# Gate and up projections of a decoder block: two sums of weight blocks come out of accumulating DMAs, and one attention step holds back its weight splits

## The chip, the core and the metric

The kernel runs on one core of one Trainium2 chip. It computes one whole decoder block in float32. The metric is the device time of one execution in microseconds (us), and the number that counts is the median of several runs. Before the change it is 1122.65 us, from three runs between 1121.96 and 1122.95 us.

The engines are named as in the profile: PE is TensorE, with PEld for its weight loads, DVE is VectorE, ACT is ScalarE, POOL is GpSimd and SP is SyncE. SP and ACT issue ordinary DMAs. POOL issues those that add to their destination.

## The reference, cut to what matters

```python
h = _rmsnorm(x, g_mix_pre)                        # x: 1024 tokens of 1024 features
u_pool, q, k, v, gates = split(h @ w_in + b_in)   # 512, 512, 128, 128, 2048 features
y_pool = multiscale_pool(u_pool)                  # windows 2, 4, 8, 16, then w_pool
y_attn = sliding_window_sink_attention(rotary(q), rotary(k), v)   # window 128, 8 heads of 64
g = sigmoid(gates)
merged = g[:, :1024] * (y_pool @ w_branch_pool) + g[:, 1024:] * (y_attn @ w_branch_attn)
x = x + _rmsnorm(merged @ w_out, g_mix_post)
h2 = _rmsnorm(x, g_mlp_pre)
ff = square(relu(h2 @ w_up)) @ w_down             # 4096 features between
out = x + _rmsnorm(ff, g_mlp_post)
```

## The kernel before, in words

**Products.** Each float32 operand is split into a high part (a cast, on ACT, L101) and a low part (source minus high part, on DVE, L104). A product of two such operands is three matmuls, high by high, high by low and low by high (`PASSES`). The helper `split` (L99) records every such pair of instructions under L101 and L104, so the tiles tell them apart.

**Seven products for eight.** The gate projection (2048 features), the up projection (4096) and the down projection multiply 2 by 2 blocks with seven block products in Winograd's form. For gates and up this is the class `Pairs` (L444). A pair p holds two neighbouring tiles of 128 output features. Its weights are four blocks: A11 and A12 (first tile, first and second half of the 1024 input features) and A21 and A22 (second tile). Each block is 128 by 4 by 128. The activations are four blocks B11 to B22 (input half by token half), and T1 to T4 are sums and differences of them. The seven products are numbered as in `OPERAND` (L442): 1 is A11 by B11, 2 is A12 by B21, 4 is A22 by T4, 5 is S1 by T1, 6 is S2 by T2, 7 is S3 by T3, and 3 is S4 by B22, where before the change S1 = A21 + A22, S2 = S1 - A11, S3 = A11 - A21 and S4 = A12 - S2. One product is 4 blocks of 128 by 3 passes, or 12 matmuls of 128 by 512.

**Where the sums are made.** `load` (L453) fetches one feature tile, 512 KB, on the SP queue, into a staging buffer (`st`, 3 buffers) or a `g` buffer. `operand` (L458) makes one weight operand. For products 5, 6, 7 and 3 it first adds or subtracts weight blocks on DVE: S1 at L464, S2 at L467, S4 at L471 and S3 at L474. These are four 128 by 512 operations for each pair, and there are 8 pairs of gates and 16 of up. S1 and S2 are held in a tile `ws` of the buffer group `ga` (6 buffers), which also holds gate operands (`ar`), raw activations (`xr`) and, in the up stage, operands of B22. `rest` (L505) runs products 6, 7, 5, 4 and 3 and puts the results together on DVE (L512, L519, L523, L526, L532).

**The stages.** (1) Queries, keys and values of the first tokens. (2) Attention, eight steps of 128 queries, while PE is also fed with other matmuls: `fill` (L651) takes them from the generator `others` (L613), which holds the remaining queries, keys and values and the pooling input projection (`u_half`, L571) with small products of branch weights (`wb_half`, L593). (3) Gates: products 1 and 2 of all eight pairs, then the five others pair by pair. (4) Branches, merge and `w_out`. (5) Up, pair by pair. (6) Down. (7) Output.

**What sets the order.** Stages 2 and the first part of 3 stand in `manual_schedule`: PE, DVE and ACT execute exactly in the order written there, and in the first part of the gates SP does so too. Elsewhere, and for POOL everywhere, the framework orders the instructions of each engine itself before the run, by program order and its own estimate of when operands and buffers are ready. In every case an engine's queue is in order: an instruction that waits holds up those behind it.

**The attention step.** In step n (L763 on) the program transposes and splits the probabilities (`attend_t`), starts the scores of step n + 2, makes the masked copy (`attend_own`, L387), scales step n + 1 (`softmax_scale`, L367), runs `fill(3.6)`, finishes the scores and the maximum of step n + 2 (L344, L351), transposes queries and keys of step n + 3 (`post_qkv`, L287: casts on ACT, low parts `qt` and `klo` on DVE), runs `fill(4.2)` and multiplies with the values (`attend_v`, L390, matmuls L399). `post_qkv`, `attend_t` and `attend_v` draw from three PSUM banks tagged `at`. A `u_half` normally splits the next weights at its eighth matmul (`flush(between[th])`, L586). While `held[0]` is true it only notes that this is due (L584). Before the change that holds during `fill(4.2)` and `attend_v` alone, and what is due is made right after `attend_v` (L793). In step 4 the `fill(3.6)` contains such a split: the weights of the next `u_half` (L556).

**Signs.** `build_gate` (L708) and `build_second` (L1049) make T1 to T4 on DVE. `gfin_b` (L1139), a broadcast of the last gain, is loaded at the start of the up stage. It takes one of the two buffers `bc`, and is first read after the third product of the down stage (L1306).

Of the kernel before, what the change touches and what calls it, by code (L numbers as in the profile page):

```python
# [8 lines left out]
F32 = mybir.dt.float32  # L9
# [5 lines left out]
P = 128  # L15
# [35 lines left out]
def block_kernel(ctx: ExitStack, tc, xt, x, consts, vecs, sinks, b_qkv, g_post, g_mlp_post,  # L51
# [100 lines left out]
    cp.tile([P, 40], F32, name="room")  # L152
# [291 lines left out]
    class Pairs:  # L444
# [12 lines left out]

        def operand(self, p, i):  # L458

            r0, r1_ = self.raw[2 * p], self.raw.get(2 * p + 1)  # L460
            if i in (5, 6, 3):
                if p not in self.sums:
                    self.sums[p] = ga_.tile([P, 2, 4, P], F32, tag="ga", name=nm("ws"))
                    dve.tensor_tensor(self.sums[p][:, 0], r1_[:, :4], r1_[:, 4:], ALU.add)  # L464
                src, s2 = self.sums[p][:, 0], self.sums[p][:, 1]
                if i == 6:
                    dve.tensor_tensor(s2, src, r0[:, :4], ALU.subtract)  # L467
                    src = s2
                elif i == 3:
                    src = r0[:, 4:]  # L470
                    dve.tensor_tensor(src, src, s2, ALU.subtract)  # L471
            elif i == 7:
                src = r0[:, :4]
                dve.tensor_tensor(src, r0[:, :4], r1_[:, :4], ALU.subtract)  # L474
            else:
                src = r0[:, :4] if i == 1 else r0[:, 4:] if i == 2 else r1_[:, 4:]
# [28 lines left out]
        def rest(self, p, f1, b6, b7, b5, done=(), then=None, b4=None):  # L505
# [6 lines left out]
            dve.tensor_tensor(u2, u2, b6, ALU.add)  # L512
# [10 lines left out]
            dve.tensor_tensor(f1[:, 512:], v7, b5, ALU.add)  # L523
# [8 lines left out]
            dve.tensor_tensor(u2, u2, b5, ALU.add)  # L532
# [114 lines left out]

    stream = others()
# [59 lines left out]
    def build_gate(kt, place):  # L708
# [21 lines left out]
    with tc.manual_schedule(engines={mybir.EngineType.PE, mybir.EngineType.DVE, mybir.EngineType.Activation}):  # L730
        rsqrt(r1, ssq, NT)
        act.activation(warm, r1[:, :1], AF.Exp)
# [30 lines left out]
        for n in range(NT):  # L763
# [12 lines left out]
            flush(late)  # L776
            fill(3.6)
# [15 lines left out]
            held[0] = False  # L793
            while len(held) > 1:
                flush(between[held.pop()])
# [39 lines left out]
    with tc.manual_schedule(engines={mybir.EngineType.PE, mybir.EngineType.DVE, mybir.EngineType.Activation,  # L835
# [7 lines left out]
        for p in range(NG0):  # L843
# [34 lines left out]
    for p in range(8):  # L878
# [3 lines left out]
        if p > 1:  # L882
            gt.load(2 * p)
            gt.load(2 * p + 1, g32([NK, P]) if p > 2 else None)
# [164 lines left out]
    def build_second(kt):  # L1049
# [8 lines left out]
        dve.scalar_tensor_tensor(r11, b12, gain(kt), r11, ALU.mult, ALU.subtract)  # L1058
        dve.scalar_tensor_tensor(t2, b22, gain(4 + kt), r11, ALU.mult, ALU.subtract)
        dve.scalar_tensor_tensor(t3, b22, gain(4 + kt), t3, ALU.mult, ALU.subtract)  # L1060
# [78 lines left out]
    gfin_b = bcast(g_mlp_post, D)  # L1139
# [20 lines left out]
    up.load(0)  # L1160
    up.load(1)
# [28 lines left out]
    def load_pair(p):  # L1190
        up.load(2 * p)
        up.load(2 * p + 1, g32([NK, P]))

    load_pair(1)
    up.rest(0, ga_.tile([P, S], F32, tag="ga", name="f1_first"), b6, b7, bank("at"), done=(6, 7),
            b4=bank("mm"))
    for p in range(1, NP):
# [16 lines left out]
        if p < NP - 1:  # L1214
            load_pair(p + 1)
# [8 lines left out]
    flush()  # L1224
    fpool.__exit__(None, None, None)
# [233 lines left out]
```

## Time and profile before

| | us |
|---|---|
| median of three runs | 1122.65 (1121.96 to 1122.95) |
| the profiled execution: its own time | 1122.0 |
| its span, first to last instruction | 1120.2 |
| PE busy | 1109.4, 99% of the span |
| PEld, DVE, ACT, POOL busy | 918.0, 791.5, 536.4, 62.3 |
| bytes moved by DMA | 197.41 MB, mean 176 GB/s |

The profile is one execution. Its own time is 1.8 us longer than the span, and 0.65 us below the median. The granted TensorE clock was 0.999. A row of a timeline reads: start in us, duration in us, engine, line, operation, output <- inputs, shapes, count, and in brackets the idle time of the engine just before and what ended it. A row of groups reads: line, engine, operation, tiles, shapes, count, then busy us, mean ns of one, and idle us before. A row of windows reads: the stretch, its length, busy us (and instructions) of PE, PEld, DVE, ACT and POOL, then the granted clock, the busy share of the DMA engines and GB/s. A row of DMA queues gives packets, MB, and the time of the packets as a share of 16 engines' span.

### The profile page before, as it was taken

How to read it: one execution, taken by the hardware profiler on the slowest of the kernel's cores; microseconds unless marked ns; L12 is line 12 of the kernel's file. 1: busy time of each engine (PE TensorE's matmuls, PEld its weight loads, DVE VectorE, ACT ScalarE, POOL GpSimd, SP SyncE). 2: the span in 40 equal slices, each digit the busy share in tenths (PEclk: the TensorE clock that was granted, in tenths of full speed). 3: DMA queues.
4: the chain of work that ended last, by engine and by line, in shares of the span. 5: the costliest groups of instructions: out<-in, count | busy, mean ns of one | idle time of the engine just before them, and what ended most of it. 6: DMA issues, size and time to landing. Idle time of an engine off the chain costs nothing.

```text
span 1120.2 us, 13921 instructions
## 1 busy us (share of the span) xinstructions
PE 1109.4 (99%) x5167; PEld 918.0 (82%) x5167; DVE 791.5 (71%) x1158; ACT 536.4 (48%) x904; POOL 62.3 (6%) x105
## 2 busy tenths in 40 slices
PE   9999999999999999999999999999999999999997
PEld 7888788888888888888888888888888888888885
DVE  5578767899768874448978767666547945447787
ACT  7466656445432333547545646354434445344342
POOL 0333210000000410000000000000000000000000
PEclk9999999999999999999999999999999999999999
DMA  9305669355772543323466554535597766332653
GB/s 349 136 11 137 151 145 311 131 188 207 244 252 69 189 147 127 131 100 115 159 215 252 198 209 157 188 122 182 204 365 249 248 199 188 97 99 71 208 189 109
DMA packets 82483, 197.41 MB, mean 176 GB/s; under 512 B 7152, under 2 KB 19568, under 8 KB 82416
## 3 DMA queue, kind: packets, MB, share of 16 engines
q1 hardware_dynamic: 72448, 174.78, 46.3%
q10 hardware_dynamic: 5616, 19.66, 4.6%
q0 software_dynamic: 4352, 2.10, 1.8%
q8 instruction: 40, 0.66, 0.2%
q14 instruction: 27, 0.22, 0.1%
HBM read 140.94 MB, written 55.57 MB: 175 GB/s over the span
## 4 chain that ended last, share of the span: by engine, by line
PE 92%; DVE 5%; ACT 2%; DMA 1%; issue 1%; DVEq 0%
PE mm L491 24%; PE at L491 16%; PE at L1297 15%; PE mm L1297 12%; PE mm L991 7%; PE mm L428 5%; PE mm L187 3%; PE mm L430 3%; PE mm L581 2%; PE at L196 1%; PE sc L187 1%; PE at L399 1%; PE sc L335 1%; PE mm L196 1%; PE at L1036 1%
## 5 line engine op out<-in xcount | busy, mean ns | idle before, releaser
L1297 PE MATMUL at<-ar,wh 128*128 128x512 f32 x744 | 169.6, 389 | 0.0
L1297 PEld LDWEIGHTS at<-ar,wh 128*128 128x128 f32 x744 | 139.6, 188 | 29.3 <-DVE ar L104 0.4
L1297 PE MATMUL mm<-ar,wh 128*128 128x512 f32 x576 | 131.0, 389 | 0.0
L1297 PEld LDWEIGHTS mm<-ar,wh 128*128 128x128 f32 x576 | 108.1, 188 | 22.4
L104 DVE TENSOR_TENSOR wh<-raw,wh 128x1024 fp32r<-128x1024 f32 x53 | 64.8, 1223 | 80.4 <-ACT wh L101 80.4
L101 ACT CAST wh<-raw 128x1024 fp32r<-128x1024 f32 x53 | 55.8, 1053 | 130.9 <-PE at L1297 58.6
L101 ACT CAST wh<-st 128x512 fp32r<-128x512 f32 (+1 forms) x105 | 66.4, 642 | 79.7 <-PE at L491 21.2
L104 DVE TENSOR_TENSOR wh<-st,wh 128x512 fp32r<-128x512 f32 (+1 forms) x105 | 78.2, 754 | 28.8 <-ACT wh L101 26.5
L491 PE MATMUL mm<-gr,wh 128*128 128x512 f32 x309 | 74.0, 390 | 0.0
L491 PEld LDWEIGHTS mm<-gr,wh 128*128 128x128 f32 x309 | 57.7, 188 | 11.8
L491 PE MATMUL mm<-T,wx 128*128 128x512 f32 x288 | 67.4, 389 | 0.0
L491 PEld LDWEIGHTS mm<-T,wx 128*128 128x128 f32 x288 | 54.1, 188 | 11.2
L491 PE MATMUL at<-T,wx 128*128 128x512 f32 x252 | 59.4, 389 | 0.0
L491 PEld LDWEIGHTS at<-T,wx 128*128 128x128 f32 x252 | 47.3, 188 | 9.8
L491 PE MATMUL mm<-x,wh 128*128 128x512 f32 x240 | 55.2, 389 | 0.0
L491 PEld LDWEIGHTS mm<-x,wh 128*128 128x128 f32 x240 | 45.1, 188 | 9.3
L104 DVE TENSOR_TENSOR ar<-B,ar 128x1024 fp32r<-128x1024 f32 x37 | 45.1, 1219 | 7.0 <-ACT ar L101 6.8
L581 PE MATMUL mm<-x,wh 128*128 128x512 f32 x192 | 47.8, 396 | 0.0
L101 ACT CAST ar<-B 128x1024 fp32r<-128x1024 f32 x37 | 38.9, 1050 | 9.2 <-DMA B<-in_w_dn_dram 6.3
L491 PE MATMUL at<-gr,wh 128*128 128x512 f32 x174 | 42.5, 390 | 0.0
L581 PEld LDWEIGHTS mm<-x,wh 128*128 128x128 f32 x192 | 35.2, 188 | 7.7
L491 PEld LDWEIGHTS at<-gr,wh 128*128 128x128 f32 x174 | 32.6, 188 | 7.3 <-DVE gr L104 0.5
(363 smaller groups left out, 2145.1 us busy)
## 6 DMA issues: line engine op xcount, KB each, us to landing
raw<-f_dram SPq DMA_DIRECT2D x53, 512.0 KB, 3.8
f_dram<-g SPq DMA_DIRECT2D x30, 512.0 KB, 3.3
B<-in_w_dn_dram SPq DMA_DIRECT2D x24, 512.0 KB, 5.8
st<-in_w_up_dram SPq DMA_DIRECT2D x23, 512.0 KB, 3.6
st<-in_w_g_dram SPq DMA_DIRECT2D x18, 512.0 KB, 4.2
f_dram<-g ACTq DMA_DIRECT2D x17, 512.0 KB, 2.6
g<-spill_dram SPq DMA_DIRECT2D x16, 512.0 KB, 4.6
raw<-in_w_dn_dram SPq DMA_DIRECT2D x16, 512.0 KB, 4.7
```

What stands on the lines that cost most here:

```text
L101: act.copy(hi, src)
L104: eng.tensor_tensor(lo, src, f32(hi), ALU.subtract)
L187: pe.matmul(bq, xs_[k][n // 4][:, xh, n % 4 * P:(n % 4 + 1) * P], wq[k][:, h, :], start=k == 0 and j == 0, stop=k == NK - 1 and j == 2)
L196: pe.matmul(bkv_of(n), xs_[k][n // 4][:, xh, n % 4 * P:(n % 4 + 1) * P], wkv[k // 2][:, h, k % 2, :], start=k == 0 and j == 0 and not (joi ...
L335: pe.matmul(sb[:, kv, i, :nk], qt[r, qx, m * P:(m + 1) * P], kx[r, k0:k0 + nk], start=j == 0, stop=j == 2)
L399: pe.matmul(flat(yb), v[:, kv, :], flat(p[:, 4 * kv:4 * kv + 4]), start=j == 0, stop=j == len(mms) - 1)
L428: pe.matmul(bs[th], whi[:, k, :], rhs(k, hl, th), start=k == 0 and hl == 0, stop=False)
L430: pe.matmul(bs[th], wlo[:, k, :], rhs(k, 0, th), start=False, stop=k == nk - 1)
L491: pe.matmul(b, w[:, wh, kt, :], xo[kt][:, xh, :], start=not after and kt == 0 and j == 0, stop=kt == 3 and j == 2, skip_group_check=after)
L581: pe.matmul(b, (whi, wlo)[h][:, k, :], xr(k, xh, th), start=j == 0, stop=j == len(mms) - 1)
L991: pe.matmul(obs[n][dj], l, wos[k][whl][:, dj * 512:(dj + 1) * 512], start=k == 0 and hl == 0 and whl == 0, stop=k == NK - 1 and hl == 1)
L1297: pe.matmul(bs[t], fo[fh][:, k2, t * P:(t + 1) * P], wo_[wh][:, k2, :], start=not after and s2 == 0 and k2 == 0 and j == 0, stop=s2 == NS ...
```

## The change

Three things are changed.

The weight loads: `load_sums(p)` lets POOL issue three DMAs. The first writes A21 twice into both halves of a `ws` tile (512 KB written), the second adds A22 to one half (256 KB) and the third adds A11 to the other (256 KB). This gives S1 = A21 + A22 and S3 = A11 + A21 without DVE. `load_pair` loads A11 and A12 as before, but of the second feature tile only A22. S2 = S1 + A11 and S4 = A12 + S2 stay on DVE. `load_sums` is called two pairs ahead. The signs that come out otherwise go into T1 to T4, with a column of negated gains (`ngain`, two 128 by 8 operations at the start of attention), and into the subtractions in `rest`.

The buffers: a `ws` tile now lives from `load_sums` until its last reader. The first result of up moves from `ga` to `bc`, and `gfin_b` is loaded after the last pair of up.

The attention step: in step 4 `held[0]` is also true during `fill(3.6)` and until after `post_qkv(7)`.

```diff
+    ngain = cp.tile([P, 16], F32, name="ngain")
         def load_sums(self, p):
+            if 2 * p + 1 >= self.src.shape[0]:
+                return
+            q = self.sums[p] = ga_.tile([P, 2, 4, P], F32, tag="ga", name=nm("ws"))
+            a21 = self.src[2 * p + 1][:, :4]
+            pool.dma_start(q, a21.unsqueeze(1).broadcast_to([P, 2, 4, P]))
+            pool.dma_start(q[:, 1], self.src[2 * p + 1][:, 4:], accum_op=ALU.add)
+            pool.dma_start(q[:, 0], self.src[2 * p][:, :4], accum_op=ALU.add)
+        def load_pair(self, p, t=None):
+            self.load(2 * p)
+            t = stage([NK, P]) if t is None else t
+            nc.sync.dma_start(t[:, :4], self.src[2 * p + 1][:, 4:])
+            self.raw[2 * p + 1] = t
         def operand(self, p, i):
-            r0, r1_ = self.raw[2 * p], self.raw.get(2 * p + 1)
-            if i in (5, 6, 3):
-                if p not in self.sums:
-                    self.sums[p] = ga_.tile([P, 2, 4, P], F32, tag="ga", name=nm("ws"))
-                    dve.tensor_tensor(self.sums[p][:, 0], r1_[:, :4], r1_[:, 4:], ALU.add)
-                src, s2 = self.sums[p][:, 0], self.sums[p][:, 1]
-                if i == 6:
-                    dve.tensor_tensor(s2, src, r0[:, :4], ALU.subtract)
-                    src = s2
-                elif i == 3:
-                    src = r0[:, 4:]
-                    dve.tensor_tensor(src, src, s2, ALU.subtract)
-            elif i == 7:
-                src = r0[:, :4]
-                dve.tensor_tensor(src, r0[:, :4], r1_[:, :4], ALU.subtract)
+            r0, r1_, q = self.raw[2 * p], self.raw.get(2 * p + 1), self.sums.get(p)
+            if i == 6:
+                src = r1_[:, 4:]
+                dve.tensor_tensor(src, q[:, 1], r0[:, :4], ALU.add)
+            elif i == 3:
+                src = r0[:, 4:]
+                dve.tensor_tensor(src, src, r1_[:, 4:], ALU.add)
...
 -            dve.tensor_tensor(u2, u2, b6, ALU.add)
+            dve.tensor_tensor(u2, b6, u2, ALU.subtract)
...
-            dve.tensor_tensor(f1[:, 512:], v7, b5, ALU.add)
+            dve.tensor_tensor(f1[:, 512:], v7, b5, ALU.subtract)
...
-            dve.tensor_tensor(u2, u2, b5, ALU.add)
+            dve.tensor_tensor(u2, b5, u2, ALU.subtract)
...
+    def release():
+        held[0] = False
+        while len(held) > 1:
+            flush(between[held.pop()])
...
-        dve.tensor_tensor(a0, a1, a0, ALU.subtract)
-        dve.scalar_tensor_tensor(a1, b1, gb, a1, ALU.mult, ALU.subtract)
-        dve.scalar_tensor_tensor(b1, b1, gb, a0, ALU.mult, ALU.subtract)
+        dve.tensor_tensor(a0, a0, a1, ALU.subtract)
+        dve.scalar_tensor_tensor(a1, b1, ngain[:, 4 + kt:5 + kt], a1, ALU.mult, ALU.add)
+        dve.scalar_tensor_tensor(b1, b1, gb, a0, ALU.mult, ALU.add)
...
         rsqrt(r1, ssq, NT)
+        for i, col in enumerate((V_G, V_GM)):
+            dve.tensor_scalar(ngain[:, 8 * i:8 * i + 8], vec[:, col:col + 8], -1.0, None, ALU.mult)
...
             flush(late)
+            held[0] = n == 4
             fill(3.6)
...
             if n + 3 < NT:
                 post_qkv(n + 3)
+            release()
...
             held[0] = True
             fill(3.0 if n == NT - 1 else 4.2)
             attend_v(n)
-            held[0] = False
-            while len(held) > 1:
-                flush(between[held.pop()])
+            release()
...
             if p + 5 < NG0:
                 gt.load(2 * p + 10)
-            elif p < 5:
-                gt.load(p - 3)
+            elif p == 3:
+                gt.load_sums(0)
+            elif p == 4:
+                gt.load_pair(0)
             elif p == 6:
-                gt.load(2)
-                gt.load(3, g32([NK, P]))
+                gt.load_pair(1, g32([NK, P]))
+                gt.load_sums(1)
...
-        if p > 1:
-            gt.load(2 * p)
-            gt.load(2 * p + 1, g32([NK, P]) if p > 2 else None)
+        gt.load_sums(p + 2)
+        if 1 <= p < 7:
+            gt.load_pair(p + 1, g32([NK, P]) if p > 1 else None)
...
-    gfin_b = bcast(g_mlp_post, D)
...
-    up.rest(0, ga_.tile([P, S], F32, tag="ga", name="f1_first"), b6, b7, bank("at"), done=(6, 7),
+    up.load_pair(1, g32([NK, P]))
+    up.load_sums(2)
+    up.rest(0, bcp.tile([P, S], F32, tag="bc", name="f1_first"), b6, b7, bank("at"), done=(6, 7),
...
         if p < NP - 1:
-            load_pair(p + 1)
+            up.load_pair(p + 1, g32([NK, P]))
+        up.load_sums(p + 2)
...
     flush()
+    gfin_b = bcast(g_mlp_post, D)
```

More of the change, by code (lines that the diff above doesn't have):

```diff
@@ L151, in block_kernel @@
     eps_y = cp.tile([P, NT], F32, name="eps_y")
-    cp.tile([P, 40], F32, name="room")
+    ngain = cp.tile([P, 16], F32, name="ngain")
+    cp.tile([P, 24], F32, name="room")
     snk = cp.tile([P, NH], F32, name="snk")
@@ L511, in rest @@
                 self.mm(b6, p, 6)
-            dve.tensor_tensor(u2, u2, b6, ALU.add)
+            dve.tensor_tensor(u2, b6, u2, ALU.subtract)
             if p in self.b1:
@@ L1057, in build_second @@
         act.activation(t3, b12, AF.Identity, scale=gain(kt))
-        dve.scalar_tensor_tensor(r11, b12, gain(kt), r11, ALU.mult, ALU.subtract)
-        dve.scalar_tensor_tensor(t2, b22, gain(4 + kt), r11, ALU.mult, ALU.subtract)
-        dve.scalar_tensor_tensor(t3, b22, gain(4 + kt), t3, ALU.mult, ALU.subtract)
+        dve.scalar_tensor_tensor(r11, b12, ngain[:, 8 + kt:9 + kt], r11, ALU.mult, ALU.add)
+        dve.scalar_tensor_tensor(t2, b22, gain(4 + kt), r11, ALU.mult, ALU.add)
+        dve.scalar_tensor_tensor(t3, b22, ngain[:, 12 + kt:13 + kt], t3, ALU.mult, ALU.add)
         dve.tensor_tensor(r21, r21, t2, ALU.subtract)
@@ L1159, in block_kernel @@
     up.prepare(4)
-    up.load(0)
-    up.load(1)
+    up.load_sums(0)
+    up.load_pair(0)
+    up.load_sums(1)
     def first_kt(kt):
```

8 lines of the change are left out of this document (3 added, 5 removed).

## The prediction

> **What bounds the kernel now.** I first read the page's busy times and its chain that ended last, then the chain in order of time, and then who made PE wait.
>
> ```profile
> PE 1109.4 (99%) x5167; PEld 918.0 (82%) x5167; DVE 791.5 (71%) x1158; ACT 536.4 (48%) x904; POOL 62.3 (6%) x105
> PE 92%; DVE 5%; ACT 2%; DMA 1%; issue 1%; DVEq 0%
> ```
> ```profile
> 636.72 19.04 PE mm L491 x84
> ...
> 789.04 19.04 PE mm L491 x84
> ```
> ```profile
> PE at L399 <- DVE qt L104: 1.5, 1, 1.5
> PE sc L335 <- DVE s L344: 0.3, 1, 0.3
> ```
>
> PE is busy for 99% of the span, and the chain is PE for 92%. A busy matmul may still be a slow one, so I look at the pace: a pair of up is 84 matmuls in 19.04 us, 0.2267 us each, and nine such pairs follow each other from 636.72 to 808.08 us without a gap (the first and the last are shown). The number of matmuls does not change, so in that stretch no DVE work that goes away can shorten anything. Apart from a wait at the very start, only two waits of PE are listed: 1.5 us and 0.3 us. What the change can win lies in such places, and not in its 33 us of DVE work (worked out below).
>
> **The attention step.** The 1.5 us are in step 4. These are the DVE, PE, ACT and SP rows around it.
>
> ```profile
> 127.19 0.68 DVE L589 TENSOR_TENSOR u<-mm,rb_all 128x512 f32<-128x512 f32 x1
> 127.79 1.22 DVE L104 TENSOR_TENSOR wh<-st,wh 128x1024 fp32r<-128x1024 f32 x1
> 128.92 0.73 DVE L344 COPY_PREDICATED s<-cst,sc 128x512 f32<-128x512 uint32 x1
> ...
> 131.22 0.68 DVE L104 TENSOR_TENSOR qt<-at,qt 128x512 fp32r<-128x512 f32 x1
> 131.82 0.28 DVE L104 TENSOR_TENSOR klo<-at,khi 128x128 fp32r<-128x128 f32 x1
> 132.02 0.68 DVE L589 TENSOR_TENSOR u<-mm,rb_all 128x512 f32<-128x512 f32 x1
> ```
> ```profile
> 129.83 0.61 PE L399 MATMUL at<-s,dv 128*128 128x512 f32 x2
> 131.96 0.73 PE L399 MATMUL at<-s,v 128*128 128x512 f32 x2 [1.51 <-DVE qt L104]
> ```
> ```profile
> 123.17 1.05 ACT L101 CAST wh<-st 128x1024 fp32r<-128x1024 f32 x1
> 131.34 0.21 ACT L359 ACTIVATE es<-es 128x8 f32<-128x8 f32 x1 [5.47 <-DVE es L353]
> 137.72 1.16 ACT L567 ACTIVATE wh<-st,vec 128x1024 fp32r<-128x1024 f32 x1
> 139.96 0.59 ACT L337 COPY s<-sc 128x512 f32<-128x512 f32 x1 [1.09 <-PE sc L335]
> ```
> ```profile
> 129.03 0.34 SPq L562 DMA_DIRECT2D st<-in_w_bp_dram  x1
> ```
> ```profile
> DMA to landing us min/median/max: 3.5/4.6/10.0
> ```
>
> PE has finished the first half of `attend_v` and needs a third `at` bank, which DVE empties with `qt`. At PE's pace the next matmul was due at 129.83 + 2 x 0.2267 = 130.28; it came at 131.96, a loss of 1.68 us. The DVE rows follow each other start to end, so `qt` is late because DVE is full, and among the rows ahead of it stands the weight split `wh` at 127.79. It takes 128.92 - 127.79 = 1.13 us of the queue. Held until after `post_qkv(7)`, it stands behind `klo`. `qt` then starts at 130.09, PE goes on at 130.83, and 0.55 us of the loss are left: **-1.13 us**. The bounds are 0 (something else is late at once) and 1.68 (all of it).
>
> What is moved with it: the cast at 123.17 (1.05 us) goes into ACT's idle 5.47 us before 131.34, where it hides. The DVE split takes the place behind `klo`, at 130.89 to 132.11, and the L589 behind it starts about when it did, at 132.05; so DVE is not late against the old time, only 1.13 us closer to PE. The low part is read by the second part of a `u_half` whose first 16 matmuls use the high part alone, so PE needs it at the earliest some 3.6 us (16 x 0.2267) after that half begins. The SP queue: L562 at 129.03 waits for the staging buffer which this split reads, so it now goes out at about 132.1, and lands at the median of 4.6 us at 136.7. Its reader on ACT, L567, would be there at 137.72 - 1.13 = 136.6. Queued behind it on ACT is the copy L337, which had waited 1.09 us for PE. A lateness of 0.1 us disappears in that, so I take 0; with the longest landing of that line, 10.0 us, it would be 142.1, 5.5 us late, of which 1.09 are covered.
>
> **The added negated gains.** Two 128 by 8 operations are put before the first queries.
>
> ```profile
> 38.80 0.17 DVE L253 TENSOR_SCALAR nsnk<-snk 128x8 f32<-128x8 f32 x1 [2.87 <-DMA snk<-in_sinks_dram]
> 48.41 0.69 DVE L104 TENSOR_TENSOR qt<-sc,qt 128x512 fp32r<-128x512 f32 x1 [4.04 <-ACT qt L101]
> ```
>
> At 0.17 us each they make 0.34 us, and DVE then stands idle for 4.04 us before 48.41: 0. Without that cover they would cost 0.34.
>
> **The sums on DVE.** Of four additions for each pair two go; S1 and S2 stand here for the four.
>
> ```profile
> L467 DVE TENSOR_TENSOR ws<-ws,st 128x512 f32<-128x512 f32 x24 | 16.5, 689 | 0.4
> L471 DVE TENSOR_TENSOR st<-st,ws 128x512 f32<-128x512 f32 x24 | 16.5, 687 | 0.3
> ```
>
> 24 pairs x 2 x 0.688 = 33 us of 791.5 of DVE. They count only where PE waits for DVE. In the gates there is one such place, at the first pair's products.
>
> ```profile
> 209.25 0.69 DVE L467 TENSOR_TENSOR ws<-ws,st 128x512 f32<-128x512 f32 x1
> ...
> 211.84 0.68 DVE L474 TENSOR_TENSOR st<-st,st 128x512 f32<-128x512 f32 x1
> 213.21 0.69 DVE L104 TENSOR_TENSOR wh<-st,wh 128x512 fp32r<-128x512 f32 x1 [0.69 <-ACT wh L101]
> 213.82 0.69 DVE L104 TENSOR_TENSOR gr<-xr,gr 128x512 fp32r<-128x512 f32 x1
> ```
> ```profile
> 214.13 0.39 PE L491 MATMUL at<-T,wh 128*128 128x512 f32 x1
> 214.56 0.73 PE L491 MATMUL at<-gr,wh 128*128 128x512 f32 x2
> 215.13 0.40 PE L491 MATMUL at<-T,wh 128*128 128x512 f32 x1
> ```
>
> One matmul takes 0.43 us from start to start and two take 0.57, where 0.23 and 0.45 are the pace: 0.32 us lost, waiting for the low parts `gr`. Ahead of `gr` on DVE two of these additions disappear, 1.4 us. So this loss goes: **-0.3 us** (bounds 0 and 0.32). In up I take 0: the pace above leaves nothing.
>
> **The sums by DMA.** POOL's last DMA of attention goes out at 179.72 (below). The first sum needs two landings in a row after that; at the longest landing quoted, 10.0 us, it is ready at 180.7 + 20 = 200.7, and DVE needs it where S1 stood, before 209.25. Were it late, DVE's hand-written order would hold the splits and builds behind it, and PE soon after. All later sums are asked for two pairs ahead. POOL's waits, for a landing or for a `ga` buffer, hold up only the next sums. Three sums and three gate operands now fill the six `ga` buffers, so the split for product 6 of the next gate pair waits until PE has done product 6 of this one; that is 48 matmuls, 10.9 us, before it is needed, against a cast and a subtraction of under 0.7 us each: 0. The late `gfin_b` has more than two products of the down stage (87 us at 192 matmuls each) before its first reader: 0. The price in DMA time is less sure.
>
> ```profile
> 179.72 1.01 POOL L404 DMA_DIRECT2D y_dram<-yt  x1 [7.48 <-issue]
> ```
> ```profile
> q1 hardware_dynamic: 72448, 174.78, 46.3%
> q0 software_dynamic: 4352, 2.10, 1.8%
> ```
> ```profile
> 226.02:253.22 27.20, 27.20 (x122) 22.52 (x121) 26.03 (x41) 12.70 (x19) 0.00 (x0) 1.00 0.59 196
> 280.42:307.62 27.20, 27.20 (x122) 22.52 (x121) 20.38 (x28) 11.19 (x14) 0.00 (x0) 1.00 0.70 245
> ```
>
> SP's queue took 46.3% of 16 x 1120.2 us for 72448 packets: 115 ns for 2.4 KB, or 97 ns for 2 KB. POOL's, whose transfers all add into y in DRAM, took 74 ns for 0.48 KB, or 314 ns for 2 KB. A pair adds 1 MB on POOL's queue, which is 512 pieces of 2 KB over 16 engines, and drops 0.25 MB on SP's. So the engines get 3.1 to 10.1 us more for each pair, less 0.8. I take the SP price for the plain copy and twice that for the adding half, which also reads its destination: 4.7 - 0.8 = 3.9 us. A pair of gates lasts 13.6 us with the engines 59% to 70% busy, so 4.1 to 5.6 us are free. By that it fits, closely: 0 for PE. An up pair has 19.04 us and more room.
>
> **Sum.** -1.13 - 0.3 + 0 = -1.43 us. The profiled execution took 1122.0 us (its span of 1120.2 and 1.8 around it), so it would be 1120.6. It lies 0.65 below the median of 1122.65, so the median becomes **1121.2 us**, 0.13% less. With the bounds of these terms alone it is 1120.4 to 1122.7. A difference of 0.2%, 2.2 us, is about what a measurement here can tell from no change: above 1124.9 is slower, below 1120.4 faster.
>
> **The rivals.**
>
> The hold nets nothing (chance 0.12): the change doesn't do what it says, because the order of DVE turns out otherwise or another operation holds the bank. Against it stands that DVE's order is written by hand there. For it: DVE's rows stay full up to 132.7. 1122.3 to 1122.7.
>
> The DMA engines become the bound in the gates (0.15): slower. With POOL's packet price of 314 ns, 9.3 us more stand against some 4.9 free, so 4.4 us are missing for each of the six pairs whose sums fall into 226 to 308 us: 26 us, of which one pair's time of lead, 13.6 us, hides; PE waits 13 us, and the median is 1135. It decides from (4.9 + 0.8) x 16 / 512 = 178 ns for a piece of 2 KB; my estimate is 145. Against it: the 314 ns come from pieces of 0.5 KB, where a fixed part weighs most. [...]
>
> The weights of L562 come late (0.05): at a landing of 10.0 us instead of 4.6, the 4.4 us not covered reach PE: 1125.6. It decides from a landing of about 5.6 us.
>
> PE has room that DVE relief opens (0.08): faster. [...] As a mechanism of this kernel: DVE has 5% of the chain, 56 us, and if it shrinks as DVE's work does, by 33 / 791.5, that is 2.3 us more, or 1118.9. Against it stand the nine pairs at an even 0.2267 us.
>
> **How the numbers follow.** The forecast has 0.60, the rivals 0.12, 0.15, 0.05 and 0.08. Faster: 0.08 and the low edge of the forecast, 0.06, make 0.14. Slower: 0.15 and a little of L562's, 0.01 (most landings that would hurt cost less than the longest), make 0.16. Within 0.2%: 0.70. The range from 1120.0 to 1124.6 leaves out the DMA rival and part of the fast one, and it takes in a landing that costs up to 3 us.
>
> **What would show it.** In the profile after: PE's wait at L399 in step 4 is near 0.4 us instead of 1.51, with `wh` behind `klo` on DVE; no slow matmuls near 214; 48 additions on DVE in place of 96; 72 DMAs on POOL's queue; pairs of up still 19.04 us. I am wrong if gate pairs take longer than 13.6 us, if the chain shows DMA in gates or up, or if ACT waits at L567 for its load by more than 1 us.

## The result, and the profile after

The changed kernel takes 1136.82 us (median of four runs, 1135.3 to 1137.46), and the kernel before takes 1122.49 us beside it. The ratio is 1.0126, with a 95% interval from 1.0108 to 1.0143. The forecast was 1121.2 us with a range from 1120.0 to 1124.6, so it failed by 15.6 us and on the other side. The profiled execution took 1137.46 us with a span of 1135.7.

In this part the lines are those of the changed file: PE's matmuls of gates and up are L501 (L491 before), POOL issues the first load of a sum buffer at L465 and the two adding DMAs at L466 and L467, DVE adds at L480 (S2, product 6) and L483 (S4), and evacuates products 7 and 5 at L529 and L533. SP loads A22 at L472.

The page after, with busy times, the two big DMA queues, and the chain that ended last:

```profile
PE 1114.1 (98%) x5167; PEld 920.7 (81%) x5167; DVE 763.9 (67%) x1112; ACT 537.4 (47%) x904; POOL 122.8 (11%) x177
...
q1 hardware_dynamic: 72448, 168.48, 43.8%
q0 software_dynamic: 14720, 27.27, 11.7%
...
PE 85%; DMA 6%; DVE 5%; ACT 2%; issue 1%; DVEq 0%; ACTq 0%; SPq 0%
```

DVE has 27.6 us less to do (791.5 before), and that bought nothing. PE lost 7 points of the chain, and DMA went from 1% to 6%. The view of who made PE wait says where:

```profile
PE at L501 <- DVE z L529: 4.5, 1, 4.5
PE mm L501 <- DVE g L529: 4.1, 1, 4.1
PE mm L501 <- DVE z L533: 2.0, 1, 2.0
...
PE mm L501 <- DVE g L533: 1.1, 1, 1.1
PE at L400 <- DVE qt L104: 0.4, 1, 0.4
```

Four new waits, 11.7 us together, all of them for an evacuation on DVE, two in the gates (`z` results) and two in up (`g` results). The wait of the attention step is down from 1.5 to 0.4 us. DVE in the gates, at the first two:

```profile
262.13 0.69 DVE L480 TENSOR_TENSOR g<-ws,st 128x512 f32<-128x512 f32 x1 [3.20 <-DMA ws<-in_w_g_dram]
262.74 0.68 DVE L104 TENSOR_TENSOR wh<-g,wh 128x512 fp32r<-128x512 f32 x1
263.35 0.68 DVE L104 TENSOR_TENSOR wh<-st,wh 128x512 fp32r<-128x512 f32 x1
263.95 0.68 DVE L533 TENSOR_TENSOR z<-z,mm 128x512 f32<-128x512 f32 x1
...
279.04 0.69 DVE L480 TENSOR_TENSOR g<-ws,st 128x512 f32<-128x512 f32 x1 [4.76 <-DMA ws<-in_w_g_dram]
279.65 0.68 DVE L529 TENSOR_TENSOR z<-g,at 128x512 f32<-128x512 f32 x1
```

The two adds are those of pairs 6 and 7. They stand in DVE's queue ahead of L533 of pair 3 and L529 of pair 4, the pairs that PE is in, and their sums have not landed. DVE idles for 3.20 and 4.76 us with the evacuations behind it, and PE with it:

```profile
259.79 0.84 PE L501 MATMUL mm<-T,wh 128*128 128x512 f32 x3
260.47 2.20 PE L501 MATMUL mm<-gr,wh 128*128 128x512 f32 x9
264.68 3.06 PE L501 MATMUL mm<-x,wh 128*128 128x512 f32 x12 [2.00 <-DVE z L533]
...
273.69 2.20 PE L501 MATMUL at<-gr,ar 128*128 128x512 f32 x9
280.38 1.65 PE L501 MATMUL at<-T,wh 128*128 128x512 f32 x3 [4.49 <-DVE z L529]
```

The last row shows a second cost. Three matmuls take 1.65 us, and three such at 259.79 took 0.84: after the wait of 4.49 us PE ran at about half its pace for a while (the last section has the granted clock there). Why the sums are late is to be seen on POOL:

```profile
250.25 0.74 POOL L465 DMA_DIRECT2D ws<-in_w_g_dram  x1 [6.77 <-DVE ar L104]
257.85 0.87 POOL L466 DMA_DIRECT2D ws<-in_w_g_dram  x1 [6.86 <-DMA ws<-in_w_g_dram]
258.43 1.19 POOL L467 DMA_DIRECT2D ws<-in_w_g_dram  x1
265.64 0.74 POOL L465 DMA_DIRECT2D ws<-in_w_g_dram  x1 [6.02 <-DVE ar L104]
271.32 0.86 POOL L466 DMA_DIRECT2D ws<-in_w_g_dram  x1 [4.94 <-DMA ws<-in_w_g_dram]
```

A first load waits until DVE has made the last split out of an older `ws` tile, however early the program asks for it. Then the adds wait for it to land. From 250.25 until DVE could start at 262.13 are 11.9 us, and from 265.64 to 279.04 are 13.4, while a pair of gates takes 13.6.

In up the item that is late is another one. SP, ACT and DVE there, in this order:

```profile
608.00 0.33 SPq L456 DMA_DIRECT2D st<-in_w_up_dram  x1
...
610.21 1.71 SPq L472 DMA_DIRECT2D g<-in_w_up_dram  x1
```
```profile
606.82 1.06 ACT L1033 ACTIVATE st<-st 128x1024 f32<-128x1024 f32 x1 [2.55 <-DMA st<-x_dram]
...
619.55 0.62 ACT L101 CAST wh<-g 128x512 fp32r<-128x512 f32 x1 [4.54 <-DMA g<-in_w_up_dram]
```
```profile
620.20 0.69 DVE L104 TENSOR_TENSOR wh<-g,wh 128x512 fp32r<-128x512 f32 x1 [6.05 <-ACT wh L101]
...
625.22 0.68 DVE L529 TENSOR_TENSOR g<-g,mm 128x512 f32<-128x512 f32 x1
```

ACT squares a tile of x1 when its load has landed (606.82). That frees the staging buffer for SP's next weight load (608.00), and three stores and the load of A22 follow in SP's queue (610.21). A22 lands 9.3 us later. Its cast on ACT and its split on DVE wait, and L529 stands behind them; PE got it 4.1 us late.

Summed over all starts of matmuls in the trace that follow later than the pace allows, the gates lose 9.2 us (0 before), and the first pairs of up lose 7.8 (0.2 before). In exchange 1.1 us came back in attention step 4 and 0.3 at the first gate pair. That makes 15.4 of the 15.5 us between the two spans.

### The profile page after: what moved, and what is told of

It reads as the page before. It is cut to its first block, busy times and chain, and to the rows that moved or that the text cites. A ratio compares the mean times of both kernels' runs of the same rounds, so it can differ in the third digit from the quotient of the medians.

```text
span 1135.7 us, 14073 instructions
## 1 busy us (share of the span) xinstructions
PE 1114.1 (98%) x5167; PEld 920.7 (81%) x5167; DVE 763.9 (67%) x1112; ACT 537.4 (47%) x904; POOL 122.8 (11%) x177
## 3 DMA queue, kind: packets, MB, share of 16 engines
q0 software_dynamic: 14720, 27.27, 11.7%
## 4 chain that ended last, share of the span: by engine, by line
PE 85%; DMA 6%; DVE 5%; ACT 2%; issue 1%; DVEq 0%; ACTq 0%; SPq 0%
PE mm L501 21%; PE at L1315 14%; PE at L501 12%; PE mm L1315 11%; PE mm L1010 7%; PE mm L429 5%; PE mm L188 3%; PE mm L431 3%; DMA ws<-in_w_g_dram 2%; PE mm L591 2%; PE at L197 1%; DMA ws<-in_w_up_dram 1%; DMA st<-x_dram 1%; PE at L1010 1%; PE sc L188 1%
## 5 line engine op out<-in xcount | busy, mean ns | idle before, releaser
L501 PE MATMUL mm<-gr,wh 128*128 128x512 f32 x309 | 73.9, 390 | 0.0
L501 PE MATMUL mm<-T,wx 128*128 128x512 f32 x288 | 67.4, 389 | 0.0
L501 PEld LDWEIGHTS mm<-gr,wh 128*128 128x128 f32 x309 | 57.7, 188 | 11.9
L501 PEld LDWEIGHTS mm<-T,wx 128*128 128x128 f32 x288 | 54.1, 188 | 11.2
L501 PE MATMUL at<-T,wx 128*128 128x512 f32 x252 | 59.1, 389 | 0.0
L501 PE MATMUL mm<-x,wh 128*128 128x512 f32 x240 | 55.4, 390 | 2.0 <-DVE z L533 2.0
L501 PEld LDWEIGHTS at<-T,wx 128*128 128x128 f32 x252 | 47.3, 188 | 9.8
L501 PEld LDWEIGHTS mm<-x,wh 128*128 128x128 f32 x240 | 45.0, 188 | 11.8 <-DVE z L533 2.4
L501 PE MATMUL at<-gr,wh 128*128 128x512 f32 x174 | 43.7, 399 | 0.0
L501 PEld LDWEIGHTS at<-gr,wh 128*128 128x128 f32 x174 | 33.9, 195 | 7.3
```

The lines of the kernel that those rows point to most:

```text
L501: pe.matmul(b, w[:, wh, kt, :], xo[kt][:, xh, :], start=not after and kt == 0 and j == 0, stop=kt == 3 and j == 2, skip_group_check=after)
```

## The experiments

Two theories. **Order**: the planned order of DVE and ACT puts operations that wait for a DMA ahead of evacuations that PE needs, and the data come later than the plan assumes, because a sum takes two landings in series and its request waits for a buffer. **Traffic**: one more MB for each pair on POOL's queue makes every load late, whatever the order.

**The hold alone.** The kernel before with `release()` and the lines

```diff
             flush(late)
+            held[0] = n == 4
             fill(3.6)
```

> The kernel before with the hold in attention step 4 alone; weight sums as before. If the hold works by itself, as the trace after suggests (PE's loss at L400 0.57 us instead of 1.67), the time is 1.1 us under before: about 1121.4 us. If that gain came from something else in the change, it equals before, 1122.5.

Measured: 1121.33 us (before 1122.62), ratio 0.9989 (0.998 to 0.9998). PE's wait there is 0.36 us:

```profile
130.93 0.73 PE L399 MATMUL at<-s,v 128*128 128x512 f32 x2 [0.36 <-DVE qt L104]
```

The hold gives its gain by itself: 1.3 us between the medians, 0.2 to 2.2 us by the interval.

**The sums alone**: the kernel after without that line.

> The kernel after without the hold: the sums by DMA alone. If the parts add up, the whole loss and 1.1 us more: about 1137.9 us, with PE waits of 1.5 us in attention step 4, 4 to 5 us in the gates and 4 to 5 us in up. If the hold had shifted the POOL or SP queue so that the sums came late, the gate stalls would be smaller and the time below 1130.

Measured: 1137.61 us, ratio 1.0129 (1.0114 to 1.0144). PE waits 1.5 us in step 4, 4.8 and 1.0 us in the gates, and 4.3 us in up. The parts add up; the whole loss is the sums'.

**The add of product 6 put later.** A number 1.0, written after the previous pair's product-5 result, is multiplied into the add:

```diff
             if i == 6:
                 src = r1_[:, 4:]
-                dve.tensor_tensor(src, q[:, 1], r0[:, :4], ALU.add)
+                if p:
+                    dve.scalar_tensor_tensor(src, q[:, 1], due[:, p - 1:p], r0[:, :4], ALU.mult, ALU.add)
+                else:
+                    dve.tensor_tensor(src, q[:, 1], r0[:, :4], ALU.add)
...
             dve.tensor_tensor(f1[:, 512:], v7, b5, ALU.subtract)
+            dve.tensor_scalar(due[:, p:p + 1], f1[:, 512:513], 0.0, 1.0, ALU.mult, ALU.add)
```

> The kernel after, but the add of product 6 (L480) is multiplied by a 1.0 that DVE writes just after the previous pair's product-5 result, so that it cannot stand ahead of that pair's evacuations. The same DMAs and bytes. Order theory (a late sum at the head of DVE's in-order queue holds up evacuations): the gate stalls at 262 and 275 us and the slow matmuls behind the second go, 9 us, so about 1128 us; the up stalls, which start from a late load and a late store read, stay. Traffic theory (16 engines are too busy, everything that is loaded comes late): the sums come as late as before and PE waits elsewhere in the gates, about 1135 to 1137 us.

Measured: 1126.27 us, ratio 1.0041 (1.0025 to 1.0057), 10.6 us less than the kernel after. DVE and POOL of this kernel (L482 is the add, L537 the product-5 result):

```profile
273.83 0.69 DVE L537 TENSOR_TENSOR z<-z,at 128x512 f32<-128x512 f32 x1 [2.03 <-PE at L505]
274.56 0.15 DVE L538 TENSOR_SCALAR due<-z 128x1 f32<-128x1 f32 x1
274.76 0.75 DVE L482 SCALAR_TENSOR_TENSOR g<-ws,due,st 128x512 f32<-128x512 f32 x1
```
```profile
253.08 0.74 POOL L466 DMA_DIRECT2D ws<-in_w_g_dram  x1 [3.32 <-DVE ar L104]
259.42 0.87 POOL L467 DMA_DIRECT2D ws<-in_w_g_dram  x1 [5.59 <-DMA ws<-in_w_g_dram]
...
272.56 0.86 POOL L467 DMA_DIRECT2D ws<-in_w_g_dram  x1 [5.14 <-DMA ws<-in_w_g_dram]
```

The sums are asked for and land as before, one landing after the other, but the add now stands where its data are there, and DVE waits for PE instead of PE for DVE. Both gate stalls are gone, and those of up as well: there it lost 1.4 us, since anchoring one add moved the rest of the planned order too. I had expected up to stay. What is left is 4.1 us at the end of the gates and in the first branches.

**Sums that nobody reads**: products 5, 6 and 7 from the raw blocks.

```diff
-                dve.tensor_tensor(src, q[:, 1], r0[:, :4], ALU.add)
+                dve.tensor_tensor(src, r1_[:, :4], r0[:, :4], ALU.add)
...
-                       5: q if q is None else q[:, 1], 7: q if q is None else q[:, 0]}[i]
+                       5: r0[:, :4], 7: r0[:, :4]}[i]
```

> The kernel after with all its sum DMAs, but nobody reads the sums: products 5, 6 and 7 are made from the raw blocks by the same number of operations (the products are then of other operands, the sums are left out of the result). Order theory: no stalls in the gates, about 1128 us; in up it depends on whether the loads stay late: if they do, 1128, if the sums were late there too, 1121. Traffic theory: the same bytes flow, so 1135 to 1137 us.

Measured: 1143.23 us, ratio 1.019 (1.0174 to 1.0206), slower than both theories said. The experiment did not do what it was made for. An operand `ar` got the `ga` buffer of a sum that nobody reads, and ACT waited for that sum to land all the same (one row of ACT):

```profile
256.22 0.62 ACT L101 CAST ar<-st 128x512 fp32r<-128x512 f32 x1 [8.36 <-DMA ws<-in_w_g_dram]
```

So it says nothing on traffic.

**One landing.** The two adding DMAs are left out:

```diff
             pool.dma_start(q, a21.unsqueeze(1).broadcast_to([P, 2, 4, P]))
-            pool.dma_start(q[:, 1], self.src[2 * p + 1][:, 4:], accum_op=ALU.add)
-            pool.dma_start(q[:, 0], self.src[2 * p][:, :4], accum_op=ALU.add)
```

> The kernel after without its two accumulating DMAs for each pair: the first load of the sum buffer alone remains, so the two sums are left out of the result, and the order of DVE and ACT is that of the kernel after. Readers wait for one landing (6 to 9 us) instead of two in series (12 to 15 us), and POOL's queue carries half the bytes. Late-sum theory: the add of product 6 stands at the same place ahead of the evacuations, but its data land about 5 us earlier, more than the 3.20 and 4.76 us that DVE waited there, so the gate stalls go (-9 us); the up stalls, which hang on SP's loads and stores, shrink only as those loads speed up: 1122 to 1128 us. If the place in the order costs by itself, whenever the data land, 1135 to 1137 us.

Measured: 1122.99 us, ratio 1.0006 (0.9997 to 1.0016). DVE's order is that of the kernel after except in 24 rows near the second pair of up. The same place in the gates (L478 is the add, L531 the evacuation of product 5):

```profile
259.12 0.68 DVE L478 TENSOR_TENSOR g<-ws,st 128x512 f32<-128x512 f32 x1
...
261.30 0.68 DVE L531 TENSOR_TENSOR z<-z,mm 128x512 f32<-128x512 f32 x1
```

The add stands where it stood and waits for nothing. So in the gates the place in the order costs nothing when the data are there. But half of the bytes that the change added to POOL's queue are gone as well.

**The adds put aside.** To keep the bytes and spare the readers the second landing, the adds went to rows of `out`:

```diff
+            for h, b in enumerate((self.src[2 * p + 1][:, 4:], self.src[2 * p][:, :4])):
+                o = out[p % 8][:, h * 512:(h + 1) * 512].rearrange("p (k n) -> p k n", n=P)
+                pool.dma_start(o, b, accum_op=ALU.add)
```

> The kernel after, but its two accumulating DMAs for each pair add into rows of the output tensor that the end of the kernel overwrites, instead of into the sum buffer; so the two sums are left out of the result. The same source blocks go through the same queue, and readers of the buffer wait for one landing instead of two. DVE's order differs from that of the kernel after at one place in up only. Late-sum theory: as with the accumulating DMAs left out, 1123 us and no stall of PE in the gates. Traffic theory: the gates stall as in the kernel after, 1133 to 1137 us. For up, where both may act: stalls of 4 to 6 us there would be traffic's, 1.5 us those of the one landing.

Measured: 1185.67 us, ratio 1.0555 (1.0534 to 1.0576). These DMAs depend on nothing, so the framework put them all at the start of POOL's queue, where the first stage waited for POOL (PE 37.0 us for one tile of `qkv`). So the added bytes did not flow in the gates, and the run tells nothing on them there.

**The adds kept beside.** The same, but they read the sum buffer, so they keep their place:

```diff
+            for h in (1, 0):
+                o = out[p % 8][:, h * 512:(h + 1) * 512].rearrange("p (k n) -> p k n", n=P)
+                pool.dma_start(o, q[:, h], accum_op=ALU.add)
```

> The kernel after, but its two accumulating DMAs for each pair read the sum buffer, once its first load has landed, and add into rows of the output tensor that the end of the kernel overwrites; so the two sums are left out of the result. They stay on POOL's queue at the place of the real ones with as many bytes, and readers of the buffer wait for one landing instead of two. DVE's order differs from that of the kernel after in 24 rows near the second pair of up and nowhere else. Late-sum theory: no stall of PE in the gates although the engines carry as much, and 1122 to 1125 us as with one landing. Traffic theory: the gates stall as in the kernel after, 1133 to 1137 us. For up, where both may act: stalls of 4 to 6 us there would be traffic's, 1.5 us those that one landing leaves.

Measured: 1130.88 us, ratio 1.0068 (1.0053 to 1.0084), between the two. The gates lose 3.8 us instead of 9.2, up 6.0 instead of 7.8 (1.7 with one landing). ACT in this kernel:

```profile
262.55 0.62 ACT L101 CAST wh<-g 128x512 fp32r<-128x512 f32 x1 [4.34 <-DMA g<-in_w_g_dram]
...
612.95 0.62 ACT L101 CAST wh<-g 128x512 fp32r<-128x512 f32 x1 [3.67 <-DMA g<-in_w_up_dram]
```

Without a second landing ACT now waits for SP's load of A22 instead, in both stages, with DVE and PE behind it. In the gates that load landed after a median of 5.5 us here, 4.6 us in the kernel after and 3.2 us with one landing. So both theories hold a part. With the bytes kept, the second landing makes 5.4 of the 9.2 us in the gates and 1.8 of the 7.8 in up; the larger part of up, and 3.8 us of the gates, come with the added bytes, in this order of DVE and ACT. The split rests on one trace of each kernel and is as good as the stand-in: its adds read the buffer and write to DRAM.

**The squares later in up.**

```diff
-        if 4 <= p < 4 + NT:
-            square_x1(p - 4)
+        if 7 <= p < 7 + NT:
+            square_x1(p - 7)
```

> The kernel after with the eight square_x1 (load of x1, square on ACT) begun at pair 7 of up instead of pair 4. Theory of the chain in up: ACT waits for the x1 load, so SP's next weight load into that staging buffer, the stores and the A22 load behind it go out late, and ACT and DVE wait for that; without these squares in the early pairs the up stalls at 595 and 621 us and the slow matmuls after them go (about 7 us): 1130 us. If the sums alone make up late, the stalls stay: 1136 to 1137 us. The gate stalls stay in either case.

Measured: 1133.72 us, ratio 1.0093 (1.0064 to 1.0123). The stall at 595 is gone. The one at 621 is still there, 3.5 us long, and a square still stands in it: the framework moved one ahead, and ACT waits for its load (first fence) before the cast on which DVE's queue waits. Up loses 5.4 us, where the kernel after lost 7.8. The second fence is PE in the gates of the same run.

```profile
623.15 1.06 ACT L1033 ACTIVATE st<-st 128x1024 f32<-128x1024 f32 x1 [4.83 <-DMA st<-x_dram]
```
```profile
265.44 4.53 PE L501 MATMUL mm<-x,wh 128*128 128x512 f32 x12 [2.88 <-DVE z L533]
269.81 0.85 PE L501 MATMUL at<-T,ar 128*128 128x512 f32 x3
...
281.00 0.96 PE L501 MATMUL at<-T,wh 128*128 128x512 f32 x3 [2.84 <-DVE z L529]
281.80 3.55 PE L501 MATMUL at<-gr,wh 128*128 128x512 f32 x9
```

**Both together, and the add one product earlier.** First the later add with the later squares:

> s2_later and squares_late together. s2_later still lost about 1.2 us in the early up pairs and 3.4 us at the end of the gates against the kernel with the hold alone. If the early up losses come from the x1 loads, 1125.0 us; if not, as s2_later, 1126.3. Neither theory has it below 1121.3, the hold alone, since the tail of the gates is not touched.

Measured: 1125.26 us, ratio 1.0025 (1.0014 to 1.0035). That looks like the first answer, but the trace says otherwise: up loses as much as without the later squares (1.4 us both times), and the difference lies at the end of the gates (2.9 against 4.1), which I can't explain. Then, with the squares still later, the number 1.0 is written after the product-7 result and no longer after that of product 5:

```diff
             dve.tensor_tensor(v7, u2, b7, ALU.add)
+            dve.tensor_scalar(due[:, p:p + 1], v7[:, :1], 0.0, 1.0, ALU.mult, ALU.add)
```

> later_squares, with the add of product 6 tied to the previous pair's product-7 result instead of its product-5 result, one product (2.7 us) earlier on DVE. If an add that is free earlier helps the tail of the gates, where 2.7 us are still lost against the hold alone, 1123 to 1125 us; if the sums that land up to 15 us after they are asked for are not there yet, the add stands waiting ahead of the product-5 result again and the time rises above 1126.

Measured: 1123.72 us, ratio 1.0007 (0.9998 to 1.0017). The end of the gates now loses 0.8 us, and up 2.2. Windows of the gates, first of the kernel after, then of this one (stretch, length, busy us of PE, PEld, DVE, ACT and POOL, clock, share of the DMA engines, GB/s):

```profile
239.60:266.80 27.20, 25.20 (x111) 20.53 (x110) 18.41 (x29) 9.79 (x14) 5.01 (x6) 1.00 0.74 218
266.80:280.40 13.60, 9.11 (x42) 7.19 (x40) 7.04 (x11) 7.47 (x9) 1.74 (x2) 0.92 0.86 245
```
```profile
239.60:266.80 27.20, 27.20 (x122) 22.53 (x121) 18.57 (x29) 9.34 (x14) 5.01 (x6) 1.00 0.74 221
266.80:280.40 13.60, 13.60 (x62) 11.26 (x61) 11.01 (x18) 5.90 (x8) 1.75 (x2) 1.00 0.76 238
```

In the first window the DMA engines are as busy and move as many bytes, and PE has no gap. A22 landed after a median of 2.9 us in the gates of this run, with all the added bytes, against 4.6 us in the kernel after. So in the gates the added bytes cost PE little where the order leaves the loads their time; how a changed order lets the same loads land sooner is not shown. In up no version with all the bytes lost less than 1.4 us, where the kernel before lost 0.2.

**Stalls of known length.** Copies on DVE ahead of a product-7 result of the kernel before:

```diff
             v7 = f1[:, 512:] if b4 is None else f1[:, :512]
+            for _ in range(slow):
+                dve.tensor_copy(v7, b7)
```

> The kernel before with 5, 7, 9, 11 and 14 idle copies put on DVE ahead of the product-7 result in pairs 6, 8, 10, 12 and 14 of up (copies of the same PSUM bank into a buffer that is overwritten at once; the result is unchanged). PE then stands idle for roughly 1, 2.5, 4, 5 and 7 us. Clock theory: after an idle time of about 4 us and more the next 8 to 10 matmuls take 0.427 us each instead of 0.227, so these stalls cost about 1.6 to 2.0 us beyond their own length; after 1 and 2.5 us there are none. Rival: the slow matmuls after the stalls of the kernel after came from its DMA traffic; then none are slow here, since the traffic is that of before.

Measured: one run, 1124.77 us, and neither answer, since no such stall came about. The 46 copies took DVE 31.7 us, and PE did not wait for them:

```profile
L520 DVE COPY g<-at 128x512 f32<-128x512 f32 x46 | 31.7, 689 | 4.0 <-PE at L491 3.2
```

PE's order differs from that of the kernel before: the framework had put other matmuls into the gaps. Work that its plan holds was covered so; the landings of the sums were not. Up lost 0.4 us. The rest of what this one execution took longer lies at the start of the down stage, where PE waited 1.3 and 0.5 us (826.04 and 827.30) for the parts of an operand whose load came late.

**The hold and the squares later**, on the kernel before, as the candidate that beats both:

> The kernel before with the hold, and with square_x1 begun at pair 7 of up instead of pair 4. The hold alone has one loss left in the early up pairs, 0.54 us at 597, where DVE's rows follow each other without idle time. If the x1 load makes it late there, 1120.8 us; if DVE is simply full, 1121.3, as with the hold alone.

Measured: 1121.01 us against 1122.67, ratio 0.9984 (0.9975 to 0.9993). The loss of 0.54 us at 597 is gone, as the first answer had it. But that is one trace of each, and the kernel before, with its squares at the old place, lost only 0.2 us in early up, so what made the 0.54 us is not settled. Beside the hold alone (1121.33, in another comparison) the 0.3 us are within the intervals. It is the fastest version tried; the one with sums by DMA and the later add is 2.7 us slower.

## Why the prediction was wrong, point by point

**The attention step: right.** `qt` was put at 130.09 and PE's return at 130.83. DVE and PE after:

```profile
130.16 0.68 DVE L104 TENSOR_TENSOR qt<-at,qt 128x512 fp32r<-128x512 f32 x1
130.76 0.28 DVE L104 TENSOR_TENSOR klo<-at,khi 128x128 fp32r<-128x128 f32 x1
130.96 1.21 DVE L104 TENSOR_TENSOR wh<-st,wh 128x1024 fp32r<-128x1024 f32 x1
```
```profile
130.89 0.73 PE L400 MATMUL at<-s,v 128*128 128x512 f32 x2 [0.41 <-DVE qt L104]
...
214.23 2.20 PE L501 MATMUL at<-gr,wh 128*128 128x512 f32 x9
```

The term of -1.13 us measured -1.1 in the trace after, and the hold alone made -1.3 between the medians. The load behind the moved split was in time: its reader on ACT started at 136.66 us, where 136.6 was worked out. The rival that the hold nets nothing is refuted by the run with the hold alone.

**The first gate pair and the negated gains: right.** The nine matmuls from 214.23 follow each other at the pace, and nothing is late at the start of attention.

**The price in DMA time: right, but its "0 for PE" was not.** POOL's queue took 11.7% of 16 x 1135.7 us against 1.8% of 16 x 1120.2. The difference is 1803 us for 10368 packets, or 174 ns for 2.4 KB, which is 147 ns for 2 KB where 145 was estimated and 178 was the point from which the rival decided. For each of the 24 pairs it is 4.7 us of 16 engines; SP's queue saved 0.9. The engines did not run out of time: they were busy for 74% and 86% of the two windows shown. But these transfers, which fit, still made others late: the run with the adds kept beside puts 3.8 us of the gates and 4.3 us of up (6.0 less 1.7) down to the added bytes. The 1135 us of the DMA rival lie near the result by luck: it took 314 ns for 2 KB and a lack of capacity, and neither was found (on POOL's queue a piece of 0.5 KB took 75 ns in the trace after, and one of 2 KB that is added 200). What it said and the forecast denied, that the added bytes cost PE time, holds in part.

**The step that failed**: "All later sums are asked for two pairs ahead. POOL's waits, for a landing or for a `ga` buffer, hold up only the next sums." The program asks two pairs ahead, but the request goes out when a `ga` buffer comes free, and then two landings follow each other: 11.9 and 13.4 us in a stage whose pairs take 13.6. I had priced exactly this chain for the first sum, where there was time (both its landings), and not for the others. The second half of the sentence failed at its "only". I had asked what is queued behind a waiting POOL, and not what is queued behind the DVE instruction that reads the sum, because I took each add to stand where S1 and S2 stood. In the kernel before, the subtractions S2 of pairs 6 and 7 stood in pairs 4 and 5 (at 272.90 and 286.50); the adds in their place stand in pairs 3 and 4. I put that down to the new target, the free half of a raw tile, which ties the add to no buffer that PE has to release; no run tested this. That a late sum at this place makes the stalls of the gates is shown: they go when the add is moved with the same sums, and with one landing DVE no longer waits for a sum at the same place, with the bytes (adds kept beside) or without. Two of the signs of being wrong came: gate pairs over 13.6 us, and DMA on the chain in gates and up.

**"In up I take 0"** holds for the steady pairs, which still take 19.04 us, and failed for the first five, of 13.6 us. I had read the free room from a steady pair. There SP's load of A22 took up to 9.3 us after issue, with ACT's squares in the chain; runs with and without the bytes show the difference (6.0 against 1.7 us). It is not the landing alone: with the add put later, A22 took 7.8 us in the median in early up, and up lost only 1.4 us.

**The slow matmuls** were in no term. They make up most of what lies between the 11.7 us of waits and the loss of 17.0 us that the gates and up show; the rest is in small gaps.

**The rival of PE room**, that less DVE work would shorten the chain, is refuted twice: 27.6 us less on DVE gained nothing outside the two places named, and 31.7 us more on DVE cost up 0.2 us. In the window from 226.02 us that the prediction shows, weight loads are busy for 22.52 of 27.20 us, 83%, while PE has no gap: the 17% in which no weights were loaded were no room in PE.

**Two sums.** DVE's work was to fall by 33 us and fell by 27.6. Rows that follow each other on DVE are 0.68 us long but start 0.60 us apart, and 48 x 0.60 less 0.34 for the negated gains is 28.5. And the least time by the bounds of the terms is 1122.65 - 1.68 - 0.32 = 1120.65 us, not 1120.4. Neither changes the argument.

## What to carry to other kernels

Where engines run in order and a planner sets the order, an operation that waits for a DMA is as dangerous as the first thing queued behind it: two adds that waited 3.20 and 4.76 us held up two evacuations here, and PE with them. So ask of every DMA that takes over an engine's work who reads it, what stands behind that reader, and whether anything but the data keeps the reader from being set early. Count the latency of a chain of DMAs from the moment its buffer comes free, not from the line that asks for it. A reader that is planned too early can be anchored to a result that PE needs first: here a 1.0 written by a tiny DVE operation, with the changed order that it brought, was worth 8 to 11 us (1125.26 and 1123.72 against 1133.72, and 1126.27 against 1136.82).

## What the runs showed of the hardware

After its longer waits PE was slow in these traces, and the granted clock was 0.50 there. In the fences above, 12 matmuls after a wait of 2.88 us took 4.37 us (265.44 to 269.81, where the next row of PE starts) instead of 2.72, and in the trace after single ones took 0.427 us from start to start instead of 0.227. These are windows of two such slow stretches, the first in the kernel after, the second in the run with the squares later:

```profile
278.15:284.98 6.83, 4.59 (x11) 3.63 (x12) 5.94 (x8) 0.97 (x2) 0.00 (x0) 0.50 0.77 248
282.36:285.77 3.41, 3.41 (x10) 2.64 (x9) 3.41 (x5) 1.01 (x2) 0.00 (x0) 0.50 0.53 190
```

The granted clock was 0.50 in both, and in the second the DMA engines were less busy (0.53) than in the full-speed window above (0.76), so the traffic did not make these matmuls slow. In the kernel after the clock was 0.50 from 278.15 to 284.98 us, around the restart at 280.38 after a wait of 4.49 us, and from 626.31 to 629.72 us, just behind the restart at 625.96 after one of 4.15 us. It was 1.00 beside the waits of 2.00 us (262.5 to 268) and 1.14 us (590 to 602).

The table has waits of PE ahead of matmuls of gates and up, from the timelines of five runs, and the time from the restart to the start of the 13th matmul, which is 2.72 us at the pace:

| run, restart at | wait, us | 12 matmuls, us |
|---|---|---|
| kernel after, 280.38 | 4.49 | 4.98 |
| kernel after, 625.96 | 4.15 | 4.44 |
| sums that nobody reads, 264.77 | 3.97 | 5.28 |
| adds kept beside, 619.36 | 3.44 | 4.31 |
| sums that nobody reads, 613.68 | 3.06 | 4.39 |
| squares later, 265.44 | 2.88 | 4.37 |
| squares later, 281.00 | 2.84 | 4.14 |
| kernel after, 264.68 | 2.00 | 2.89 |
| adds kept beside, 265.15 | 1.78 | 2.90 |
| one landing, 612.73 | 1.46 | 2.85 |
| kernel after, 596.78 | 1.14 | 2.85 |

After the waits of 2.84 us and more these 12 matmuls took 1.4 to 2.6 us more than at the pace, after those of 2.00 us and less 0.1 to 0.2. None of these waits lies between 2.00 and 2.84 us, so a limit is not shown. One wait of 1.79 us, at a place not listed here, was followed by seven slow matmuls all the same, so the length alone does not decide in these traces.

The packet records of the trace after give the price of adding. A first load (512 KB written) is 128 packets of 4 KB, 185 ns each; a DMA that adds 256 KB into SBUF is 128 packets of 2 KB, 200 ns each. So adding a block took the DMA engines little more time (25.6 us) than writing it twice (23.6 us). For 2 KB that is 92 and 200 ns, where the prediction took 97 and 194. That the reading of the destination makes the adding half dearer was the author's estimate; the runs show its price alone. The 174 ns further up are an average that also counts 16 packets of 4 bytes for each DMA.
